# Attention in blocks of 64 queries, with two heads to an operand, and the last two operands of the recurrent projection split in place

## The chip, the cores and the metric

The kernel runs on one core of a Trainium2 chip. The metric is the device time of one execution in microseconds (us); before and after are compared by medians of several runs. In the profile the engines are called PE (TensorE, matrix multiplication; PEld is its weight load), DVE (VectorE), ACT (ScalarE), POOL (GpSimd) and SP (the engine that only issues transfers). Transfers (DMAs) between the core's memory (SBUF) and the device's memory (HBM) are issued from the queues of SP, POOL and, rarely, ACT. TensorE writes its results to PSUM.

## What is computed

One residual block of a decoder on 1024 tokens of width 1024, all in float32. Cut to what matters here:

```python
proj = h @ w_in[l]
q, k, v, g_attn, xr, g_rnn, m_attn, m_rnn = jnp.split(proj, SPLIT_POINTS, axis=-1)
# q: 16 heads of 64, k and v: 4 heads of 64; both q and k are rotated by position
s = jnp.einsum('bnqkgd,bnskd->bnkgqs', qb, kb) * (1.0 / math.sqrt(hd))
band = (diff >= 0) & (diff < WINDOW)            # a query sees itself and 127 keys before
s = jnp.where(mask[None, :, None, None], s, -1e30)
m = jnp.maximum(jnp.max(s, axis=-1, keepdims=True), sink)
p = jnp.exp(s - m)
denom = jnp.sum(p, axis=-1, keepdims=True) + jnp.exp(sink - m)
o = jnp.einsum('bnkgqs,bnskd->bnqkgd', p / denom, vb)
...
y_rnn = rg_lru(xr, ...) * jax.nn.silu(g_rnn)    # a linear recurrence over the tokens
merged = (jax.nn.sigmoid(m_attn) * (y_attn @ w_attn_proj[l])
          + jax.nn.sigmoid(m_rnn) * (y_rnn @ w_rnn_proj[l]))
x = x + gate[:, None, :] * (merged @ w_out[l])
return rmsnorm(x, final_g)
```

## The kernel before

Every float32 product is made of three: each operand is split into a high piece (a copy in the type float32r, made on ACT) and a low piece (the remainder, a subtraction on DVE), and high x high, high x low and low x high are summed in PSUM. The names end in `h` and `l` (`hh`, `hl`, `wh`, `wl`, `yh`, `yl`).

The order of the work on each engine is written by hand: the program text is the order of each queue, SP's and POOL's too. An engine that meets an instruction whose input isn't there waits, and all that follows on it waits too.

First come the normalization and the values' projection. Then `run` (L818) walks through 23 `pairs` of 256 output columns of the input projection, seven slots each, every slot 12 matmuls of 512 columns. What becomes of a pair's result is told by its "sinks": queries and keys are rotated, split and stored to HBM (`rope_a` L603, `rope_b` L620, which holds the pieces in tiles `rhi` and `rlo` of two buffers each); merge gates go through tanh and are stored (`tanh_sinks` L792); the recurrent input is convolved and goes through `after_gates` (L1003), whose steps `a1` to `d7` end in `y`, split and stored in `yh_d`, `yl_d` for each of eight channel blocks c (two to each `hb`, 0 to 3). Work that isn't tied to a slot waits in three lists (`waiting`, L651) and is put in where DVE and ACT have room by their declared costs: among it `v_prep` (L1190), which splits the values and stores them in `vs_d` and `dv_d` (the latter holds the difference of a block of 128 tokens and the one before), and `out_weights` (L1159), eight blocks of four steps that prepare the weights of the last product in the tiles `wq`. What of these is left when the attention begins goes to `rest_out` (L1593) and is put in by `outs` (L1596).

When slot 155 of the last pair is done, the attention starts: a loop over u = 0 to 34 (L1626). A unit u is 128 queries of one group of four heads that share a key head; eight units make a group, and the first of each (u % 8 == 0) has no keys before its own. The pass u of the loop emits, in this order on each engine: the scores of unit u (`scores` L1264, PE), their copy (`maxima_a`, ACT), the masked copy and the maximum (`maxima_d`, DVE), the exponentials of unit u-1 (`weights_a`, ACT), a piece of other TensorE work (what is left of the last pair, then the projection of the recurrent branch in `rp_steps` L1411: 12 matmuls of 512 columns in either case), the division (`weights_d`, DVE), the values of unit u-3 (`values` L1338, PE, with `join_a` on ACT and `join_d` on DVE), the transposes of the weights of unit u-2 (PE) and their split (`split_a` ACT, `split_d` DVE), and the masked copies of the two pieces (`masks` L1326, POOL). PSUM holds one buffer each for scores, transposes and values.

Scores of a unit are four heads x two terms: the stationary operand is one head's 128 queries (high and low pieces stacked to 128 rows), the moving operand 256 keys. The window is kept in a circular layout: the weights of the 256 keys are folded to 128 columns, key j of the block before and key j of the own block never being seen by the same query. So values are `vs` of the block before with the whole weights, and the difference `dv` with the masked ones:

```python
prods = [((vs if n else dv)[:, n % 2, :], m) for m in full]
prods += [(dv[:, n % 2, :], m) for m in masked]
```

each a matmul of 512 columns (four heads x 128 queries): four for a unit, two for a group's first.

The projection of the recurrent branch takes `y` from HBM by `load_y` (L1394), c = 0, 1 into tiles that held operands of the pairs (`hh[0..3][0]`), c = 2 to 5 into `whole`, c = 6, 7 into a pool of its own. After the loop follow the rest of this projection, the attention's projection, the merge and the last product. The tail works on the same tiles in both versions.

## Time and profile before

| what | us |
|---|---|
| three runs | 909.07, 910.93, 910.11 |
| median | 910.11 |
| the profiled run, its time | 909.08 |
| the profiled run, its span in the trace | 907.4 |

The span is what the trace covers; the 1.7 us around it are start and end. The profile's page gives, for each engine, busy time and share of the span; then the span in 40 slices; the queues; the chain of work that ended last, followed back from the last instruction; the costliest groups of instructions. Views of the trace by group, by tile, by window and in order of time give the rest. A line such as `L1274 PE MATMUL s_ps<-ks,qs 128*128 128x256` names the line of the kernel, engine, operation, output and inputs, and the shape. The ends of matmuls in the trace are modelled, so their starts and counts say more than their busy time. Loop and stages in the profiled run: pairs from 91.7 us, attention loop from 560.4 us to about 732 us, the rest to 907.4.

### The profile page before, as it was taken

Reading aid. Unit: us, or ns where it says so; the run is one execution under the profiler, and the core shown is the slowest. Engines: PE = TensorE matmul, PEld = TensorE weight load, DVE = VectorE, ACT = ScalarE, POOL = GpSimd, SP = SyncE. Lnnn points to the kernel's source line nnn. Section 1 sums busy time; section 2 is a strip of 40 time slices with the busy share of each in tenths; the row PEclk is TensorE's granted clock in tenths of the full one; section 3 lists DMA queues with packets and bytes.
Section 4 is the critical chain, followed back from the end, with each engine's and each line's share of the span. In section 5 each row is a group of like instructions: output and inputs, shape, how many; then the busy total and the mean of one; then the engine's idle time right before and its main releaser. Section 6 shows DMA issues by size and latency. Waiting matters only on the chain.

```text
span 907.4 us, 12605 instructions
## 1 busy us (share of the span) xinstructions
PE 889.1 (98%) x4171; PEld 739.2 (81%) x4171; DVE 725.8 (80%) x1158; ACT 554.9 (61%) x1097; POOL 124.7 (14%) x204
## 2 busy tenths in 40 slices
PE   5999999999999999999999999999999999999997
PEld 3879888878888788878887888888888888888885
DVE  7988799698669974987698476899999846779875
ACT  6754675455556745774767685888888731114555
POOL 0120000000110000000100001354443421310002
PEclk9999999999999999999999999999999999999999
DMA  9951786862534360345345257996666258879314
GB/s 348 404 203 68 253 272 223 294 219 97 180 121 151 130 218 24 129 155 180 107 155 183 85 194 254 328 370 211 214 201 212 85 182 322 315 272 346 110 47 186
DMA packets 88882, 182.57 MB, mean 201 GB/s; under 512 B 14049, under 2 KB 30433, under 8 KB 88818
## 3 DMA queue, kind: packets, MB, share of 16 engines
q1 hardware_dynamic: 82192, 162.09, 51.8%
q0 software_dynamic: 6336, 19.37, 5.9%
q8 instruction: 33, 0.54, 0.3%
q10 hardware_dynamic: 290, 0.32, 0.1%
q14 instruction: 31, 0.25, 0.1%
HBM read 125.01 MB, written 57.12 MB: 201 GB/s over the span
## 4 chain that ended last, share of the span: by engine, by line
PE 86%; DVE 6%; DMA 3%; ACT 2%; issue 2%; SPq 0%; POOL 0%; DVEq 0%; ACTq 0%
PE bk L696 41%; PE rp L174 14%; PE bo L1857 7%; PE pmain L174 6%; PE pgate L992 5%; PE s_ps L1274 3%; PE pv L1346 3%; DMA r<-w_main 2%; PE pt L1312 2%; PE bk L174 1%; DVE wl L110 1%; PE bk L1520 1%; PE bk L1519 1%; PE bk L1518 1%; DMA wada<-w_ss 1%
## 5 line engine op out<-in xcount | busy, mean ns | idle before, releaser
L696 PE MATMUL bk<-nh,wl 128*128 128x512 f32 x368 | 143.9, 391 | 0.5 <-DVE wl L110 0.4
L696 PE MATMUL bk<-nh,wh 128*128 128x512 f32 x368 | 143.4, 390 | 0.0
L696 PE MATMUL bk<-nl,wh 128*128 128x512 f32 x368 | 143.2, 389 | 0.0
L696 PEld LDWEIGHTS bk<-nh,wl 128*128 128x128 f32 x368 | 69.1, 188 | 16.7 <-DVE wl L110 2.1
L696 PEld LDWEIGHTS bk<-nh,wh 128*128 128x128 f32 x368 | 69.1, 188 | 14.4 <-ACT rhi L626 0.2
L696 PEld LDWEIGHTS bk<-nl,wh 128*128 128x128 f32 x368 | 69.1, 188 | 14.4
L110 DVE TENSOR_TENSOR wl<-r,wh 128x512 fp32r<-128x512 f32 x112 | 80.1, 729 | 0.0
L60 POOL DMA_DIRECT2D wq_d<-wq x32 | 21.9, 685 | 407.2 <-DVE wq L1172 392.6
L104 ACT CAST wh<-r 128x512 fp32r<-128x512 f32 x112 | 68.0, 617 | 8.8 <-DMA r<-w_ap 5.1
L696 PE MATMUL bk<-hh,wh 128*128 128x512 f32 x184 | 71.6, 389 | 0.0
L696 PE MATMUL bk<-hh,wl 128*128 128x512 f32 x184 | 71.6, 389 | 0.0
L696 PE MATMUL bk<-hl,wh 128*128 128x512 f32 x184 | 71.6, 389 | 0.0
L110 DVE TENSOR_TENSOR wl<-ws,wh 128x512 fp32r<-128x512 f32 x80 | 54.8, 686 | 4.3 <-ACT wh L104 4.2
L104 ACT CAST wh<-ws 128x512 fp32r<-128x512 f32 x80 | 48.2, 614 | 3.3 <-PE bk L1520 2.7
L1298 ACT ACTIVATE p<-p,small 128x129 f32<-128x129 f32 x128 | 50.1, 401 | 0.0
L799 ACT ACTIVATE c<-bk 128x512 f32<-128x512 f32 x31 | 18.5, 595 | 44.0 <-PE bk L696 43.9
L696 PEld LDWEIGHTS bk<-hl,wh 128*128 128x128 f32 x184 | 34.5, 188 | 7.2
L696 PEld LDWEIGHTS bk<-hh,wl 128*128 128x128 f32 x184 | 34.5, 188 | 7.1
L696 PEld LDWEIGHTS bk<-hh,wh 128*128 128x128 f32 x184 | 34.5, 188 | 7.1
L1857 PE MATMUL bo<-wh,sum 128*128 128x512 f32 x128 | 39.6, 389 | 0.0
L1274 PE MATMUL s_ps<-ks,qs 128*128 128x256 f32 (+1 forms) x256 | 37.6, 289 | 0.0
L696 PE MATMUL bk<-hha,wl 128*128 128x512 f32 x92 | 36.1, 393 | 0.6 <-DVE wl L110 0.6
(409 smaller groups left out, 2290.1 us busy)
## 6 DMA issues: line engine op xcount, KB each, us to landing
r<-w_main SPq DMA_DIRECT2D x100, 256.0 KB, 4.3
wada<-w_ss SPq DMA_DIRECT2D x16, 512.5 KB, 9.3
qs<-q_d SPq DMA_DIRECT2D x16, 512.0 KB, 5.8
wq_d<-wq POOLq DMA_DIRECT2D x24, 256.0 KB, 2.8
wr<-wq_d SPq DMA_DIRECT2D x24, 256.0 KB, 5.0
ks<-k_d SPq DMA_DIRECT2D x24, 192.0 KB, 4.2
wq<-w_out POOLq DMA_DIRECT2D x16, 256.0 KB, 5.2
q_d<-rhi SPq DMA_DIRECT2D x16, 256.0 KB, 3.6
```

The costliest lines, as they stand in the source:

```text
L60: return eng.dma_start(dst, src)
L104: A.copy(dst[0][:], src)
L110: V.tensor_tensor(out=dst[1][:], in0=src, in1=f32(dst[0][:]), op=ALU.subtract)
L174: mm = T.matmul(ps[hf], ww, xx[kc][hf], start=(kc == 0 and ww is w_h and xx is xh), stop=(kc == KC - 1 and xx is xl))
L696: W["pe"] = T.matmul(ps, ww[:, c], b[kc][xx_], start=(first and kc == 0 and i == 0), stop=(kc == 3 and i == 2), skip_group_check=not first)
L799: A.activation(t["t"], s(), AF.Tanh, scale=0.5)
L992: W["pe"] = T.matmul(ps[:, SL[hf]], ww[:, c0:c0 + P], xx_[:, SL[hf]], start=(ic == 0 and i == 0), stop=(ic == 1 and i == 2))
L1274: W["pe"] = T.matmul(o, qs[:, j, qc], ks[:, b, k0 + (0 if n else P):k0 + 256], start=(b == 0), stop=(b == 1))
L1298: A.activation(px[:, j, :], px[:, j, :], AF.Exp, bias=sm[:, 0, j:j + 1], accum_out=sm[:, 1, j:j + 1])
L1312: W["pe"] = T.transpose(pt[:, j, :], px[:, j, 0:P], ident[:])
L1346: W["pe"] = T.matmul(pv[:], b, m[:].rearrange("p j q -> p (j q)"), start=(i == 0), stop=(i == len(prods) - 1))
L1857: T.matmul(bank[p][i] if dst is None else dst, a[:, ts_], b[:][:, sl], start=(new and kc == 0 and j == 0), stop=(kc == 3 and j == 2), skip ...
```

## The change

It has two parts.

The attention works in blocks of 64 queries. A unit is still 128 queries of four heads, but a stationary operand of the scores holds two heads x 64 queries, and its moving operand is the 192 keys that these can see (`h` is the half of the unit). Weights are folded to 128 columns, of which only 64 need the mask. In the values, a matmul has 256 columns (two operands of one half): four with the whole weights' pieces, and two with `cm`, in which the masked 64 rows of the high and of the low piece are stacked. The first unit of a group leaves out those that see no keys. For this, queries lie in HBM by blocks of 64 tokens (`q_d`) and are stored from POOL's queue in runs of 64 floats, values lie by blocks of 64 with two blocks of zeros in front (`vs_d`), and four transfers from POOL's queue load them instead of two. The merge gates' stores are all issued from POOL.

In the last two blocks of the recurrent branch (c = 6, 7), `y` isn't split and stored: `d6` writes it into the four tiles `wq`, and `y_direct` splits it into `hh`, `hl` just before and in the first pass of the attention loop. For that, `out_weights` stops after three of its eight blocks, and the load of the fourth comes at u = 26 from SP. The pieces of the recurrent projection's first two columns run over c = 6, 7, then 4, 5, then 0 to 3, and `load_y` follows that order. The tiles `yq` of the loop take turns on one tile of their own and two of `wq`.

Not shown: the mask of 64 columns in place of 128, the sinks' layout, the split of `load_kq` into `load_k` and `load_q`, and index changes in the joins.

```diff
-    vs_d = [tc.dram_tile([P, 8, P], F32, name=f"vs_d{g}") for g in range(NG)]
-    dv_d = [tc.dram_tile([P, 8, P], F32, name=f"dv_d{g}") for g in range(NG)]
+    vs_d = [tc.dram_tile([64, 18, P], F32, name=f"vs_d{g}") for g in range(NG)]
+    dv_d = [tc.dram_tile([64, 18, P], F32, name=f"dv_d{g}") for g in range(NG)]
...
-    q_d = [tc.dram_tile([512, S], F32, name=f"q_d{g}") for g in range(NG)]
+    q_d = [tc.dram_tile([16, 512, 64], F32, name=f"q_d{g}") for g in range(NG)]
...
+    zero = rpp.tile([P, HALF], F32, tag="rl", name="zero", bufs=2)
+    G.memset(zero[:, :2 * P], 0.0)
...
+    for g in range(NG):
+        dma(vs_d[g][:, 0:2, :], zero[0:64, :2 * P].rearrange("p (i c) -> p i c", i=2), G)
...
-            dma(dst[r0:r0 + P, SL[th]], t["h"][:])
-            dma(dst[r0 + 2 * P:r0 + 3 * P, SL[th]], t["l"][:])
+            for n_, r in ("h", r0), ("l", r0 + 2 * P):
+                if dst is k_d:
+                    dma(dst[r:r + P, SL[th]], t[n_][:])
+                else:
+                    dma(dst[8 * th:8 * th + 8, r:r + P, :].rearrange("x p q -> p x q"),
+                        t[n_][:].rearrange("p (x q) -> p x q", q=64), G)
...
-                        dma(dst[j][:, SL[th]], t["t"], G if "att" in W else nc.sync)
+                        dma(dst[j][:, SL[th]], t["t"], G)
...
+            if hb < 3:
+                V.tensor_tensor(out=t["rz"][:], in0=t["rz"][:], in1=t["gg"][:], op=ALU.mult)
+                return
+            for i in range(2):
+                V.tensor_tensor(out=wq[2 * oc + i][:].rearrange("p a t -> p (a t)"),
+                                in0=t["rz"][:, SL[i]], in1=t["gg"][:, SL[i]], op=ALU.mult)
...
+                [[("D", 0, 1.22, d6)]]] + ([[], []] if hb == 3 else [
+                    [[("A", 1.05, 0, a7)]], [[("D", 0, 1.22, d7)]]])
...
+                if (kc, q) == (1, 1):
+                    waiting[2].append(lambda: False)
                 waiting[2].extend(out_weights(kc, slice(q * 256, q * 256 + 256)))
...
                 dma(t[:], w_out[k * P:(k + 1) * P, :].rearrange(
-                    "p (a t) -> p a t", a=2)[:, :, cols], G)
...
-                dma(dst[g], t[d_][:])
+                for b in range(2):
+                    dma(dst[g][:, 2 + b:18:2, :], t[d_][64 * b:64 * b + 64])
...
+        dma(qs[:], q_d[g][t0 // 64:t0 // 64 + 4].rearrange("x (a j) q -> a x (j q)", j=4))
+        U["q", m] = qs
...
-        g, n0 = m // 4, (m % 4) * 2
-        vs = at.tile([P, 2, P], F32R, tag="vs", name="vs", bufs=2)
-        dv = at.tile([P, 2, P], F32R, tag="dv", name="dv", bufs=2)
-        dma(dv[:], dv_d[g][:, n0:n0 + 2, :], G)
-        lo = 0 if n0 else 1
-        dma(vs[:, lo:, :], vs_d[g][:, n0 - 1 + lo:n0 + 1, :], G)
-        U["v", m] = vs, dv
+        g, i0 = m // 4, m % 4 * 4
+        vb = at.tile([P, 4, P], F32R, tag="vb", name="vb", bufs=2)
+        vd = at.tile([P, 4, P], F32R, tag="vd", name="vd", bufs=2)
+        for e in range(2):
+            half = slice(64 * e, 64 * e + 64)
+            dma(vb[half], vs_d[g][:, i0 + e:i0 + e + 4, :], G)
+            dma(vd[half], dv_d[g][:, i0 + 2:i0 + 6, :], G)
+        U["v", m] = vb, vd
...
-        qc = slice((n % 2) * P, (n % 2 + 1) * P)
-        k0 = (n % 2) * P
+        ks, qs = U["k", u // 2], U["q", u // 2]
         s_full = psx.tile([P, 1024], F32, tag="s", name="s_ps")
         s_ps = s_full[:].rearrange("p (j k) -> p j k", j=4)
         for j in range(4):
-            o = s_ps[:, j, :] if n else s_ps[:, j, P:]
+            h = j // 2
+            t0 = (n % 2) * P + 64 * h
+            first = 0 if n else P - 64 * h
+            w = qs[:, n % 2 * 2 + h, j % 2 * P:j % 2 * P + P]
             for b in range(2):
-                W["pe"] = T.matmul(o, qs[:, j, qc], ks[:, b, k0 + (0 if n else P):k0 + 256],
+                W["pe"] = T.matmul(s_ps[:, j, first:192], w, ks[:, b, t0 + first:t0 + 192],
                                    start=(b == 0), stop=(b == 1))
         U["s", u] = s_ps, *U.pop(("p", u))
         if n % 2 and u // 2 + 2 < 16:
-            load_kq(u // 2 + 2)
+            load_k(u // 2 + 2)
+            load_q(u // 2 + 2)
...
         s_ps, px, sm = U["s", u]
-        A.copy(px[:, :, 0:P], s_ps[:, :, P:])
+        if u % 8:
+            A.copy(px[:, :, 0:P], s_ps[:, :, 0:P])
+        else:
+            A.copy(px[:, :, 0:64], s_ps[:, :, P:192])
...
-        p = px[:, :, 0:P]
+        p = px[:, :, 0:64]
         if u % 8:
-            V.copy_predicated(p, W["mgt"][:].unsqueeze(1).to_broadcast([P, 4, P]),
-                              s_ps[:, :, 0:P])
+            V.copy_predicated(p, W["mle"][:].unsqueeze(1).to_broadcast([P, 4, 64]),
+                              s_ps[:, :, P:192])
         else:
-            G.affine_select(out=p, in_=p, pattern=[[0, 4], [-1, P]], compare_op=ALU.is_ge,
-                            fill=-1e30, base=0, channel_multiplier=1)
+            G.memset(px[:, 0:2, 64:P], -1e30)
+            for e in range(2):
+                o = p[64 * e:64 * e + 64]
+                G.affine_select(out=o, in_=o, pattern=[[0, 4], [-1, 64]],
+                                compare_op=ALU.is_ge, fill=-1e30, base=0,
+                                channel_multiplier=1)
...
     def masks(u):
-        phc, plc = U["m", u]
-        ms = []
-        if u % 8:
-            for s_, tag in ((phc, "phm"), (plc, "plm")):
-                d_ = at.tile([P, 4, P], F32R, tag=tag, name=tag)
-                G.affine_select(out=d_[:], in_=f32(s_[:]), pattern=[[0, 4], [1, P]],
-                                compare_op=ALU.is_ge, fill=0.0, base=0,
-                                channel_multiplier=-1)
-                ms.append(d_)
-        U["m", u] = [phc, plc], ms
+        pieces = U["m", u]
+        cm = at.tile([P, 4, P], F32R, tag="cm", name="cm")
+        for i, s_ in enumerate(pieces):
+            G.affine_select(out=cm[64 * i:64 * i + 64].rearrange("p g (e q) -> p (g e) q", e=2),
+                            in_=f32(s_[0:64]).rearrange("p g (e q) -> p (g e) q", e=2),
+                            pattern=[[0, 8], [1, 64]], compare_op=ALU.is_ge, fill=0.0, base=0,
+                            channel_multiplier=-1)
+        U["m", u] = *pieces, cm
...
-        n = u % 8
-        vs, dv = U["v", u // 2]
-        full, masked = U.pop(("m", u))
-        prods = [((vs if n else dv)[:, n % 2, :], m) for m in full]
-        prods += [(dv[:, n % 2, :], m) for m in masked]
-        pv = psx.tile([P, 4 * P], F32, tag="v", name="pv")
-        for i, (b, m) in enumerate(prods):
-            W["pe"] = T.matmul(pv[:], b, m[:].rearrange("p j q -> p (j q)"),
-                               start=(i == 0), stop=(i == len(prods) - 1))
-        U["pv", u] = [pv[:].rearrange("p (a e q) -> p a e q", a=2, e=2)]
-        if n % 2 == 0 and u // 2 + 1 < 16:
+        vb, vd = U["v", u // 2]
+        phc, plc, cm = U.pop(("m", u))
+        pv = psx.tile([P, 4, P], F32, tag="v", name="pv")
+        prods = [(vb, m, h) for m in (phc, plc) for h in range(0 if u % 8 else 1, 2)]
+        prods += [(vd, cm, h) for h in range(2)]
+        for i, (b, m, h) in enumerate(prods):
+            js = slice(2 * h, 2 * h + 2)
+            W["pe"] = T.matmul(pv[:, js, :], b[:, u % 2 * 2 + h, :], m[:, js, :],
+                               start=(i == 0), stop=(i >= len(prods) - 2),
+                               skip_group_check=True)
+        if u % 2 == 0 and u // 2 + 1 < 16:
             load_v(u // 2 + 1)
...
-            W["yq"] = at.tile([P, 2, 256], F32, tag="yq", name="yq", bufs=3)
+            W["yq"] = (at.tile([P, 2, 256], F32, tag="yq", name="yq") if u % 6 == 0 else
+                       wq[1 + u % 6 // 2])
...
+    def y_direct(c):
+        j = 2 * (c - 6)
+        yh[c], yl[c] = [[t[j + i][0] for i in range(2)] for t in (hh, hl)]
+        for i in range(2):
+            src = wq[j + i][:].rearrange("p a t -> p (a t)")
+            later_a.append(lambda i=i, src=src: A.copy(yh[c][i], src))
+            later_d.append(lambda i=i, src=src: V.tensor_tensor(
+                out=yl[c][i], in0=src, in1=f32(yh[c][i]), op=ALU.subtract))
+
+    Y_ORDER = (4, 5, 0, 1, 2, 3)
+
+    def load_y(n):
+        c = Y_ORDER[n]
+        if n < 4:
+            h_, l_ = whole["hh", n + 4], whole["hl", n + 4]
...
             for kc in (2 * kc2, 2 * kc2 + 1):
                 W["pe"] = mm_k([rp_acc[c % 2][:, t] for t in SL], (O.get((c, 0)), O.get((c, 1))),
-                               kc, xh=yh, xl=yl)
+                               kc, xh=yh, xl=yl, first=0 if c > 1 else 6,
+                               last=KC - 1 if c > 1 else 3)
...
-        seq = [(c, k) for k in range(4) for c in range(2)]
+        seq = [(c, k) for k in (3, 2, 0, 1) for c in range(2)]
         seq += [(c, k) for c in range(2, KC) for k in range(4)]
-        load_y(3)
+        load_y(1)
...
             if i in (0, 1, 2, 3):
-                load_y(i + 4)
...
-    at_slot(s_last + 2, [("N", 0, 0, lambda: load_r(0)), ("N", 0, 0, lambda: load_y(0))],
-            ("N", 0, 0, lambda: load_y(1)), ("N", 0, 0, lambda: load_r(1)), [],
-            [("N", 0, 0, lambda: prep_r(0, 0)), ("N", 0, 0, lambda: load_y(2))],
-            ("N", 0, 0, lambda: prep_r(1, 0)))
+    y_direct(6)
+    do_later()
+    at_slot(s_last + 2, [("N", 0, 0, lambda: load_r(0)), ("N", 0, 0, lambda: y_direct(7))],
+            [], ("N", 0, 0, lambda: load_r(1)), [],
+            [("N", 0, 0, lambda: prep_r(0, 1)), ("N", 0, 0, lambda: load_y(0))],
+            ("N", 0, 0, lambda: prep_r(1, 1)))
...
+            if u == 0:
+                load_k(1)
+                load_q(1)
+                load_v(0)
...
+        if u == 26:
+            outs(1)
```

More of the change, by code (lines that the diff above doesn't have):

```diff
@@ L174, in mm_k @@
                 mm = T.matmul(ps[hf], ww, xx[kc][hf],
[L175 to L176 removed]
+                              start=(kc == first and ww is w_h and xx is xh),
+                              stop=(kc == last and xx is xl))
         return mm
@@ L1644, in tile_hybrid_block @@
             join_a(u - 3)
+        if u >= 3:
             join_d(u - 3)
```

77 lines of the change are left out of this document (38 added, 39 removed).

## The prediction

> **What bounds the kernel.** The page's busy table comes first, then its chain of waits by engine: TensorE is busy for nearly the whole span, and most of the chain that ends last runs through it.
>
> ```profile
> PE 889.1 (98%) x4171; PEld 739.2 (81%) x4171; DVE 725.8 (80%) x1158; ACT 554.9 (61%) x1097; POOL 124.7 (14%) x204
> PE 86%; DVE 6%; DMA 3%; ACT 2%; issue 2%; SPq 0%; POOL 0%; DVEq 0%; ACTq 0%
> ```
>
> Busy time of pipelined matmuls is no measure of a stage, so I read the chain in order of time where the change works: the loop over 32 units (u = 0 to 31; four of them, u = 0, 8, 16, 24, are the first of their group). Columns: start us, length us, group.
>
> ```profile
> 672.06 0.95 PE s_ps L1274 x8
> 673.01 2.75 PE rp L174 x12
> 675.75 0.91 PE pv L1346 x4
> 676.66 0.44 PE pt L1312 x4
> 677.10 0.84 PE s_ps L1274 x8
> 677.94 2.82 PE rp L174 x12
> 680.77 0.91 PE pv L1346 x4
> 681.68 0.44 PE pt L1312 x4
> 682.11 0.95 PE s_ps L1274 x8
> ...
> 695.90 0.46 PE pv L1346 x2
> ```
>
> One pass is scores (0.95), a piece of the projection (2.75), values of an earlier unit (0.91) and transposes (0.44): 672.06 to 677.10 is 5.04 us, the four pieces sum to 5.05, and nothing is between them. The unit at 677.10 is a first one, with 128 score columns instead of 256; the 0.46 at 695.90 is a first unit's values, two matmuls instead of four. So here time is TensorE's own work, and what the change takes from it counts, as long as the others keep up. The view by stages (us; busy and count for PE, PEld, DVE, ACT, POOL; clock, DMA share, GB/s) says how near they are:
>
> ```profile
> 663.00:688.00 25.00, 25.00 (x141) 21.52 (x140) 22.95 (x43) 19.94 (x66) 13.72 (x22) 1.00 0.61 193
> ```
>
> DVE 92%, ACT 80%, POOL 55%. The clock is 1.00: no gain or loss from there.
>
> **Values.** A 512-column matmul costs 0.91 / 4 = 0.228 us, a 256-column one 0.95 / 8 = 0.119. Four of the first become six of the second (two halves with each of the high and low pieces, two with the masked pieces stacked into one operand): 6 x 0.119 = 0.714, a gain of 0.197, of which I take 0.19. A first unit goes from 0.46 to 4 x 0.119 = 0.476, a loss of 0.02.
>
> **Scores.** Eight matmuls remain, of 192 columns instead of 256. By the rows, eight of 128 columns cost 0.84 (0.105 each), so below 256 columns the pitch hardly falls: the weight load of each sets it. And the first unit doesn't keep even that: its projection piece is 2.82 instead of 2.75, so the two together are 3.66 against 3.70, a gain of 0.04. With 192 columns the gain lies between 0 (the 256 row) and 0.11 (the 128 row, without the late projection). I take 0.03, near what the whole 128-column unit showed. The first units' scores are short already: nothing.
>
> Here the Trainium skill has two rules ("TensorE: Matmul & The Clock Gate"). Its section "Back-to-back issue gap" gives a warm matmul N / 2.4 + 2.5 ns, an estimate of 82 ns for 192 columns; its section "LDWEIGHTS (loading the stationary operand)" gives 128 columns of weights 128 / 1.2 = 107 ns. The trace agrees with the second (0.105), which speaks against this part of the change; by the first alone it would gain 8 x (0.119 - 0.082) = 0.29 per unit.
>
> **Does the gain reach the end?** The loop drains at its end:
>
> ```profile
> 716.97 0.03 ACTq L1317
> ...
> 719.45 1.03 POOL plm L1332
> 720.48 0.04 issue
> 720.52 0.50 PE pv L1346
> ```
>
> From 716.97 to 720.52 TensorE waits for one unit's copy, split and mask; three of its four values matmuls run in that gap and only the last is exposed. Afterwards four of six do and two are exposed, so that unit's values gain nothing. Sum: 27 x (0.19 + 0.03) + 0.03 - 4 x 0.02 = 5.9 us.
>
> **What must keep up.** Groups by form between 607 and 688 us (busy us, mean ns, idle before and its cause), and two of one tile (shortest, median, longest ns) for the slope by size:
>
> ```profile
> L1288 DVE COPY_PREDICATED p<-mgt,s_ps 128x512 f32<-128x512 uint32 x15 | 11.1, 738 | 0.0
> L1293 DVE TENSOR_REDUCE small<-p 128x4 f32<-128x516 f32 x17 | 11.7, 691 | 3.0 <-POOL p L1291 1.1 <-DVE p L1288 0.5
> L1355 ACT COPY ob<-pv 64x256 f32<-64x256 f32 x17 | 6.3, 369 | 14.0 <-PE pv L1346 6.5 <-issue 6.1 <-ACT p L1298 1.5
> L1332 POOL TENSOR_SCALAR_AFFINE_SELECT plm<-plc 128x512 fp32r<-128x512 f32 x14 | 14.0, 1002 | 9.3 <-DVE plc L1323 9.3
> L1332 POOL TENSOR_SCALAR_AFFINE_SELECT phm<-phc 128x512 fp32r<-128x512 f32 x14 | 9.1, 652 | 11.3 <-ACT phc L1317 11.3
> L60 POOL DMA_DIRECT2D dv<-dv_d x8 | 4.4, 554 | 0.0
> ...
> L1172 DVE TENSOR_TENSOR wq<-wq,gate_bc x16: 682/689/694, 232.6 to 798.3; 128x512 f32<-128x512 f32 x16
> L1177 DVE TENSOR_TENSOR wq<-wq x8: 417/420/424, 235.6 to 798.9; 128x256 f32<-128x256 f32 x8
> ```
>
> The new pass is 5.04 - 0.22 = 4.82. DVE's masked copy of the scores halves its columns and, by the slope 689 - 420, loses 0.27: DVE goes from 0.92 x 5.04 = 4.63 to 4.36, 90% of the new pass. ACT keeps its 4.02 (0.80 x 5.04), 83%, and stood idle 14.0 us over 17 units for the join copy, 0.8 each, against the 0.22 that go. POOL's two masks keep 512 elements per partition, on half the partitions; a bound of 0 and of the longer row, 1.0, each. It gets four loads of values instead of two in every second unit, 2 x 0.55 = 1.1 us, and in each first unit two masks that weren't there (1.65) and three short operations for one: 2.8 of a pass at 55% becomes 3.3 of 4.82. What counts is when the mask is ready:
>
> ```profile
> 649.37 1.02 POOL L1332 TENSOR_SCALAR_AFFINE_SELECT plm<-plc 128x512 fp32r<-128x512 f32 x1 [0.37 <-DVE plc L1323]
> 651.50 0.39 PE L1346 MATMUL pv<-plm,dv 128*128 128x512 f32 x1
> ```
>
> It ends at 650.39 and is used at 651.50: 1.1 us of cover, more than the 0.22. So none of these costs anything; with the cover gone each us of lateness would be paid 32 times.
>
> **What moves.** The last two operands (channels 6 and 7) lose two stores and two loads each way through memory, and two ACT and two DVE operations in the recurrent stage; four ACT copies and four DVE subtractions of 512 columns (0.69 each) come at the loop's start, 2.8 us on DVE. That engine waits there:
>
> ```profile
> 562.85 0.69 DVE L1293 TENSOR_REDUCE small<-p 128x4 f32<-128x516 f32 x1 [5.40 <-POOL p L1291]
> ```
>
> 5.4 us idle before it covers them: nothing, at most 0.7 for one that comes late. The other operands keep their distance to their use (the order of loads and of the pieces is permuted together). Of the output weights only one load moves, from POOL in mid-kernel to SP at unit 26, long before its use: nothing.
>
> **Queues.** Queries (32 stores) and merge-gate stores leave SP's queue for POOL's, and query stores become runs of 256 bytes, 1024 in a store. SP's view, then two slices by stages, a wait and issue times:
>
> ```profile
> 163.90 5.58 SPq L60 DMA_DIRECT2D sma_d<-c  x2
> 169.53 0.93 SPq L60 DMA_DIRECT2D r<-w_main  x2
> ...
> 170.00:180.00 10.00, 10.00 (x46) 8.29 (x45) 6.30 (x20) 3.94 (x8) 0.00 (x0) 1.00 0.98 339
> 180.00:190.00 10.00, 9.83 (x41) 7.17 (x40) 9.52 (x17) 6.16 (x11) 0.00 (x0) 1.00 0.38 135
> ...
> 131.78 0.38 SPq L60 DMA_DIRECT2D q_d<-rhi  x1
> 146.76 0.32 SPq L60 DMA_DIRECT2D q_d<-rhi  x1
> ...
> L60 POOL DMA_DIRECT2D wq_d<-wq x32: 562/725/742, 233.6 to 800.7; - x32
> ACT rhi L626 <- DMA q_d<-rhi: 8.9, 4, 4.1
> ```
>
> On the good side: weight loads that stood behind two waiting gate stores went out at 169.53, and in 180 to 190 TensorE started 41 matmuls, not 46: 5 x 0.228 = 1.1 us that may go. On the bad side: POOL takes 0.56 us for a store of 128 runs and 0.74 for one of 256, so 1024 runs are, as an estimate, 0.56 + 7 x 0.18 = 1.8 us; no row shows such a store on POOL (bounds 0.56 and, at twice the slope, 3.1). Eight of them, one group's, take 14.6 us, and two groups start 131.78 and 146.76, 15.0 us apart: it just fits. Behind a late store wait ACT and DVE, which need its two buffers back, as ACT does already (8.9 us in four times), and behind them the weights. I take 0 for both together (bounds: 1.1 gained, 15 lost).
>
> **Sum.** The profiled run took 909.08 (span 907.4); the median of three, 910.11, is 1.0 above it. 909.08 - 5.9 = 903.2, and from the median **904.2**.
>
> **The rivals.**
> 1. *The scores run at column rate.* Columns cost (0.228 - 0.119) / 256 = 0.42 ns, so 192 would be 0.092, eight 0.73, a gain of 0.22 per unit instead of 0.03: 28 x 0.19 = 5.3 more, 899. The 128-column row speaks against it. The first rule of the Trainium skill's TensorE page, above, would bring 28 x (0.29 - 0.03) = 7.3 more, an estimate of 897.
> 2. *The cover is gone.* DVE at 90% is late by pieces (its slowest operations meet POOL's masks), or the mask comes after its use; half to all of the gain is lost: 906 to 910. For it: DVE and ACT feed each other in one pass. Against: DVE gains more than TensorE.
> 3. *Slower: POOL can't issue the query stores.* The point is 15.0 / 8 = 1.9 us a store. At 2.7, 24 stores of three groups are 19 us late, of which the idle share of DVE and the buffers hide perhaps a third: +13, 917. For it: the estimate lies just below the point. Against: POOL has nothing else there (0.00 busy in both slices). The Trainium skill ("SBUF — State Buffer", section "SBUF: two separate sides") says that descriptors written by GpSimd are blocked while DVE holds the shared port, 0.62 us becoming 3.1. By it such a store would pass the point easily; the trace's 32 POOL stores, 0.74 at the longest, don't show it.
> 4. *It doesn't do what it says*: the loop's pass stays 5.04, 910.
>
> **Chances.** Forecast, 901 to 906: 0.62. Rival 1 or the 1.1 us and a better start, below 901: 0.11. Rival 2: 0.13, half of it within 0.2% (1.8 us, about what a measurement of this kernel can tell from no change). Rival 3: 0.12. Rival 4: 0.02. Faster 0.80, same 0.08, slower 0.12. The range 899.5 to 908.0 leaves out rival 3, the slow end of rival 2 and a little below.
>
> **What would show it.** In the profile after, a pass of 4.8 us with eight scores at 0.85 to 0.95, six values at 0.71 and transposes at 0.44, and nothing between them. Right as to SP: 46 matmuls in the slice where 41 were. Wrong: gaps between values and transposes, waits of TensorE on DVE or POOL in the loop; POOL's query stores over 1.9 us with waits of ACT on rhi and DVE on rlo; a pass near 4.6 (rival 1).

## The result, and the profile after

The kernel after takes 914.67 us (median of 12 runs, 911.68 to 918.14), the kernel before in the same comparison 909.02 (12 runs, 907.43 to 910.93): a ratio of 1.0061, 95% interval 1.0045 to 1.0077. It is 5.6 us slower where 5.9 us faster was forecast. The profiled run took 912.4 us, 2.3 below its median, with a span of 910.7. The runs of the kernel after differ by 6.5 us, those of the kernel before by 3.5, and the longer ones have the lower granted clock: 0.998 in the run of 911.68, 0.991 in that of 918.14.

The same views as before the change, first the page's busy table and its chain by engine. (Lines have moved: scores are L1304, values L1383, transposes L1351, matmuls of the pairs L706.)

```profile
PE 885.6 (97%) x4235; PEld 739.1 (81%) x4235; DVE 720.3 (79%) x1162; ACT 554.5 (61%) x1103; POOL 191.8 (21%) x313
PE 60%; issue 12%; DVE 12%; DMA 7%; ACT 5%; POOL 4%; SPq 1%; DVEq 0%; POOLq 0%; ACTq 0%
```

TensorE's share of the chain falls from 86 to 60%; "issue" rises from 2 to 12%, DVE from 6 to 12, the transfers (DMA) from 3 to 7, ACT from 2 to 5 and POOL from 0 to 4. Yet the pass that was forecast is there, in the chain in order of time (start, length, group) and in the view by stages:

```profile
653.12 0.87 PE s_ps L1304 x8
653.99 2.77 PE rp L174 x12
656.76 0.72 PE pv L1383 x6
...
657.91 0.87 PE s_ps L1304 x8
...
661.55 0.47 PE pv L1383 x4
...
663.00:688.00 25.00, 25.00 (x156) 22.24 (x156) 22.73 (x43) 21.89 (x70) 15.12 (x28) 1.00 0.83 240
```

653.12 to 657.91 is 4.79 us, against 5.04; the values take 0.72, a first unit's 0.47, the scores 0.87. So the loss is elsewhere. To find it, take the start of the scores of each unit from TensorE's timeline; three of the 32 for the kernel before, then for the one after:

```profile
560.19 1.00 PE L1274 MATMUL s_ps<-ks,qs 128*128 128x128 f32 x8
621.86 1.19 PE L1274 MATMUL s_ps<-ks,qs 128*128 128x256 f32 x8
711.67 1.19 PE L1274 MATMUL s_ps<-ks,qs 128*128 128x256 f32 x8
```
```profile
564.93 1.00 PE L1304 MATMUL s_ps<-ks,qs 128*128 128x64 f32 x8
628.60 1.12 PE L1304 MATMUL s_ps<-ks,qs 128*128 128x192 f32 x8
715.51 1.12 PE L1304 MATMUL s_ps<-ks,qs 128*128 128x192 f32 x8
```

They are units 0, 13 and 31. "Passes 0 to 12" is the time from the first to the second of them, "13 to 30" from the second to the third. The forecast's sum (0.19 for a unit's values, 0.03 for its scores, -0.02 for a first unit's values), cut at the same places, stands beside it:

| stretch | before | after | change | forecast |
|---|---|---|---|---|
| up to the first scores | 560.2 | 564.9 | +4.7 | 0 |
| passes 0 to 12 | 61.7 | 63.7 | +2.0 | -1.8 |
| passes 13 to 30 | 89.8 | 86.9 | -2.9 | -3.5 |
| the rest of the span | 195.7 | 195.2 | -0.5 | -0.6 |

The last two rows came nearly as forecast. 9.2 us separate the profiled time from the sum, and 8.5 of them lie in the first two rows: 4.7 before the loop, 3.8 in its first thirteen passes. Each has its own cause. (The medians lie further apart than these two profiles: 5.6 us slower, not 3.3. The rows place what the profiled run lost; they don't hold the 2.3 us between it and its median.)

**Before the loop.** The stages of after, where the kernel before had 46 and 41 matmuls, and TensorE's timeline in the second of them:

```profile
170.00:180.00 10.00, 9.67 (x43) 8.01 (x44) 6.86 (x21) 4.49 (x9) 1.08 (x2) 1.00 0.77 227
180.00:190.00 10.00, 7.68 (x27) 5.85 (x26) 7.49 (x14) 4.60 (x9) 0.26 (x1) 0.83 0.55 194
```
```profile
181.12 0.39 PE L706 MATMUL bk<-nh,wh 128*128 128x512 f32 x1
183.82 0.50 PE L706 MATMUL bk<-nh,wl 128*128 128x512 f32 x1 [2.32 <-DVE wl L112]
...
185.32 0.63 PE L706 MATMUL bk<-nh,wl 128*128 128x512 f32 x1
...
188.73 0.39 PE L706 MATMUL bk<-hha,wh 128*128 128x512 f32 x1
```

TensorE waits 2.32 us for the low piece of a weight, and then, from 185.32 to 188.73, eight matmuls start 0.43 us apart instead of 0.227. Back along the chain that weight is `DMA r<-w_main`, issued at 175.48. SP's view around it, before and then after:

```profile
170.55 0.38 SPq L60 DMA_DIRECT2D vs_d<-vs  x1
171.05 0.35 SPq L60 DMA_DIRECT2D dv_d<-dv  x1
...
173.78 0.98 SPq L60 DMA_DIRECT2D r<-w_main  x1
```
```profile
170.90 1.27 SPq L60 DMA_DIRECT2D vs_d<-vs  x2
172.26 1.63 SPq L60 DMA_DIRECT2D dv_d<-dv  x2
...
175.48 2.54 SPq L60 DMA_DIRECT2D r<-w_main  x2
```

The split values go to HBM in four transfers instead of two, in runs of 512 bytes. They occupy SP for 3.0 us instead of 0.9, and the weight load behind them goes out 1.7 us later. From there to its landing it takes 7.0 us, and 6.6 before: it comes late because it is issued late. The queries' stores, which the prediction feared, take POOL 0.89 us each.

**In the loop's first passes** the chain runs through value loads, here the third pair of units:

```profile
591.12 0.57 POOL smr_d L60
591.68 0.53 POOL vb L60
592.21 0.52 POOL vd L60
...
593.23 9.06 DMA vd<-dv_d
...
602.42 0.49 PE pv L1383 x2
```

Four issues stand behind a merge-gate store on POOL, and the last of them lands 9.06 us later. Where TensorE waits in the loop (total us, times, longest), where the kernel before has one wait of 0.3 us:

```profile
PE pv L1383 <- POOL cm L1369: 1.4, 3, 0.7
PE pv L1383 <- DMA vb<-vs_d: 1.2, 1, 1.2
```

Two more, for `vd` and for a result of DVE, take 0.3 us each.

### The profile page after: what moved, and what is told of

Same layout as the page of the kernel before. It is cut to its first block, busy times and chain, and to the rows that moved or that the text cites. A ratio compares the mean times of both kernels' runs of the same rounds, so it can differ in the third digit from the quotient of the medians.

```text
span 910.7 us, 12963 instructions
## 1 busy us (share of the span) xinstructions
PE 885.6 (97%) x4235; PEld 739.1 (81%) x4235; DVE 720.3 (79%) x1162; ACT 554.5 (61%) x1103; POOL 191.8 (21%) x313
## 2 busy tenths in 40 slices
DMA packets 92917, 183.12 MB, mean 201 GB/s; under 512 B 14561, under 2 KB 39649, under 8 KB 92850
## 4 chain that ended last, share of the span: by engine, by line
PE 60%; issue 12%; DVE 12%; DMA 7%; ACT 5%; POOL 4%; SPq 1%; DVEq 0%; POOLq 0%; ACTq 0%
PE bk L706 26%; PE rp L174 12%; PE bo L1913 7%; PE pmain L174 5%; PE pgate L1002 5%; PE s_ps L1304 2%; DMA r<-w_main 2%; DVE wl L110 2%; PE pv L1383 2%; POOL q_d L60 2%; DMA wg<-posi 1%; DVE jk L251 1%; DMA vd<-dv_d 1%; PE pt L1351 1%; DVE ws L728 1%
## 5 line engine op out<-in xcount | busy, mean ns | idle before, releaser
L706 PE MATMUL bk<-nh,wl 128*128 128x512 f32 x368 | 144.6, 393 | 4.6 <-DVE wl L112 2.3
L706 PE MATMUL bk<-nl,wh 128*128 128x512 f32 x368 | 143.8, 391 | 0.0
L706 PE MATMUL bk<-nh,wh 128*128 128x512 f32 x368 | 143.7, 391 | 0.0
L706 PEld LDWEIGHTS bk<-nh,wl 128*128 128x128 f32 x368 | 69.2, 188 | 21.8 <-DVE wl L110 5.0
L706 PEld LDWEIGHTS bk<-nh,wh 128*128 128x128 f32 x368 | 69.2, 188 | 14.4
L706 PEld LDWEIGHTS bk<-nl,wh 128*128 128x128 f32 x368 | 69.4, 188 | 14.2
L706 PE MATMUL bk<-hh,wh 128*128 128x512 f32 x184 | 71.7, 389 | 0.0
L706 PE MATMUL bk<-hl,wh 128*128 128x512 f32 x184 | 71.6, 389 | 0.0
L706 PE MATMUL bk<-hh,wl 128*128 128x512 f32 x184 | 71.6, 389 | 0.0
L706 PEld LDWEIGHTS bk<-hh,wl 128*128 128x128 f32 x184 | 34.6, 188 | 7.3
L706 PEld LDWEIGHTS bk<-hh,wh 128*128 128x128 f32 x184 | 34.5, 188 | 7.1
L706 PEld LDWEIGHTS bk<-hl,wh 128*128 128x128 f32 x184 | 34.5, 188 | 7.1
L706 PE MATMUL bk<-hha,wl 128*128 128x512 f32 x92 | 36.3, 394 | 0.9 <-DVE wl L110 0.9
L706 PE MATMUL bk<-hha,wh 128*128 128x512 f32 x92 | 36.0, 392 | 0.0
```

Of the source, the lines that this page charges most:

```text
L706: W["pe"] = T.matmul(ps, ww[:, c], b[kc][xx_], start=(first and kc == 0 and i == 0), stop=(kc == 3 and i == 2), skip_group_check=not first)
```

## Experiments

Three theories for the first row of the table: V (value stores), Q-runs (256-byte runs of the query stores), Q-queue (POOL's queue for queries and gates). Three for the second: I (POOL's issue order and time), B (the doubled bytes of the value loads), L (loads issued too late); a fourth, Y (late loads of y), came up on the way. "First scores" and passes are read as above, from one profiled run each; times are medians, ratios are to runs of the kernel before on the same chip. Some profiles are of runs far from their median: e1's took 5.1 us more (914.95), e16's 4.6 less (906.33), e18's 1.5 more, and e4's 10.9 more, a run that its ratio leaves out; their stages are read with that in mind. e6, e10 and e17 leave out half of the values, so they are measures of a cause and not kernels to use. Of those that do the whole computation `e12_all` is the fastest. Runs on different chips are compared by their ratios.

| kernel | us | ratio (95%) | first scores | passes 0-12 | 13-30 |
|---|---|---|---|---|---|
| e1_v_store | 909.85 | 1.0002 (0.9980-1.0024) | 559.8 | 69.4 | 87.0 |
| e2_q_runs | 917.5 | 1.0097 (1.0069-1.0125) | 562.3 | 69.0 | 86.9 |
| e3_queues | 916.51 | 1.0073 (1.0047-1.0099) | 565.3 | 66.1 | 86.8 |
| e4_v_two | 962.47 | 1.0551 (1.0481-1.0622) | 568.6 | | |
| e5_v_early | 914.25 | 1.0052 (1.0037-1.0067) | 559.6 | 63.4 | 93.0 |
| e6_v_half | 906.96 | 0.9969 (0.9955-0.9983) | 559.2 | 62.2 | 87.0 |
| e7_v_two | 965.88 | 1.0595 (1.0547-1.0643) | 562.6 | | |
| e8_v_end | 909.2 | 0.9992 (0.9975-1.0008) | 558.7 | 65.0 | 87.1 |
| e9_v_pool | 908.73 | 0.9988 (0.9972-1.0004) | 558.2 | 63.8 | 87.3 |
| e10_half_end | 905.73 | 0.9956 (0.9940-0.9973) | 560.4 | 61.2 | 87.0 |
| e11_y_early | 909.97 | 1.0000 (0.9986-1.0013) | 558.7 | 65.6 | 87.0 |
| e12_all | 906.41 | 0.9970 (0.9959-0.9981) | 558.9 | 61.9 | 87.0 |
| e13_y | 908.49 | 0.9995 (0.9981-1.0009) | 559.1 | 65.3 | 87.0 |
| e14_end | 910.48 | 1.0012 (1.0000-1.0024) | 560.3 | 65.7 | 87.3 |
| e15_y_late6 | 907.47 | 0.9985 (0.9971-0.9999) | 560.0 | 62.5 | 86.9 |
| e16_y_undone | 910.95 | 1.0029 (1.0015-1.0043) | 558.3 | 63.6 | 86.9 |
| e17_all_half | 905.92 | 0.9959 (0.9945-0.9973) | 558.4 | 61.9 | 87.0 |
| e18_before_dose | 911.16 | 1.0013 (1.0002-1.0023) | 561.7 | 63.6 | 89.8 |

### The time before the loop: e1, e2, e3, e9

e1: values in HBM by whole blocks of 128 tokens again, one store each; a pair of units then needs five loads instead of four (not shown).

```diff
...
-                for b in range(2):
-                    dma(dst[g][:, 2 + b:18:2, :], t[d_][64 * b:64 * b + 64])
+                dma(dst[g][:, 1:9, :], t[d_][:])
...
```

> Of the 4.7 us that are lost before the attention loop (first scores at 560.35 before, 565.09 after). Value stores again in one transfer of 4 KB runs each (eight issues on SP instead of sixteen), five loads of values instead of four. Theory V (the stores of v in 512-byte runs hold SP and the transfers, so v and w_main land late): first scores at 561 to 562, 46 matmuls in 160-190, time 4 us under after, about 910. Theory Q (the query stores, their runs or their queue): first scores stay at 564 to 566, time that of after, 914 to 916 (the fifth load may cost some 0.5 in the loop).

e2: queries in runs of 2 KB; four transfers load them instead of one (not shown).

```diff
...
-                    dma(dst[8 * th:8 * th + 8, r:r + P, :].rearrange("x p q -> p x q"),
-                        t[n_][:].rearrange("p (x q) -> p x q", q=64), G)
+                    dma(dst[r:r + P, SL[th]], t[n_][:], G)
...
```

> Queries stored in runs of 2 KB again, still from POOL's queue; the loads take the 256-byte runs instead, four transfers for one, from SP in the loop. Theory Q-runs (256-byte runs in the stores load the transfers where queries are made): first scores at 561 to 562. Theory Q-queue (POOL's queue instead of SP's) and theory V: stay at 564 to 566. In the loop the loads may cost something; the total is then no better than after, the first scores decide.

e3: `G` taken from these stores and, up to the attention, from the merge gates'.

> Query stores (still 256-byte runs) and merge-gate stores from SP's queue again. Theory Q-queue: first scores at 560 to 562 and 4 us under after, about 910. Theories Q-runs and V: 564 to 566, 914 to 916.

Only e1 starts the loop as early as the kernel before. (e2's time is no measure here: TensorE waits 3.6 us for one of its query loads in the loop.) e3, with all the old queues, has the same event as after; its chain:

```profile
175.63 6.81 DMA r<-w_main
...
183.07 0.69 DVE wl L112
...
183.81 11.38 PE bk L706 x36
```

Q-queue falls with e3, and e2's 562.3 leaves Q-runs at most a part. But the first scores also hold what the profiled runs differ by ahead of this event: the 673rd matmul of the pairs starts at 169.73 us before, at 168.14 in after and at 170.84 in e18, which changes nothing there. The time from it to the start of the 757th leaves that out. It is 20.11 us before, 24.71 in after, 19.72 in e1, 22.72 in e2 and 24.88 in e3, so e2 keeps most of the loss too. V stays, but e1 changed both the issues and the packets. e9 takes the four stores as they are and issues them from POOL (`G` at the end of the two lines).

> After, with the four stores of values per group (512-byte runs as in after) issued from POOL's queue instead of SP's. Theory V-issue (what counts is SP's time for four issues, 0.6 us each and up, ahead of the weight loads r<-w_main): first scores at 560 to 561.5, no wait of TensorE at 183, time 909 to 911. Theory V-packets (the 512-byte packets fill the transfers and the weights land late whoever issues them): first scores at 563 to 566, time 913 to 916.

The stages of e9:

```profile
160.00:170.00 10.00, 10.00 (x46) 8.29 (x45) 8.23 (x19) 5.02 (x10) 3.86 (x7) 1.00 0.93 308
170.00:180.00 10.00, 10.00 (x46) 8.29 (x45) 8.56 (x25) 4.24 (x8) 3.26 (x5) 1.00 0.98 314
180.00:190.00 10.00, 10.00 (x46) 8.29 (x45) 9.93 (x18) 7.57 (x15) 2.67 (x3) 1.00 0.62 216
```

46 matmuls in each, and the first scores at 558.2, 2.0 us ahead of the kernel before. All profiles agree: the 84 matmuls from the 673rd to the 757th take 22.40 to 24.88 us in the five with four value stores on SP (after, e2, e3, e4, e7), 19.25 to 20.40 in the eight with two, and 19.04 in each of the seven with four on POOL.

That the stores have to leave SP is shown. e9 alone doesn't show that it is SP's time and not the packets, since the packets changed as well: on POOL's queue these stores go in packets of 4096 bytes, and the kernel's packets under 2 KB fall from 39649 to 31457. Two other things speak for SP's time. The weight load is late in after, not slow: from its issue to its landing it takes 7.0 us, in e3 and e9 6.8, before 6.6. And e3, whose query stores add some 25000 packets under 512 bytes between 100 and 200 us (29517 against 4414), loses what after loses. Whether four stores hold SP that long by their number or by their shorter runs, no run separates.

### The value loads: e4, e7, e5, e6, e8

e4 and e7: two loads of 128 partitions, whose source is written out by hand (two halves, 64 partitions each); e7 joins the 2 KB of a partition in the target, too.

```diff
-        for e in range(2):
-            half = slice(64 * e, 64 * e + 64)
-            dma(vb[half], vs_d[g][:, i0 + e:i0 + e + 4, :], G)
-            dma(vd[half], dv_d[g][:, i0 + 2:i0 + 6, :], G)
+        for t_, d_, i_, step in (vb, vs_d, i0, P), (vd, dv_d, i0 + 2, 0):
+            o = d_[g][:, i_:i_ + 4, :]
+            dma(t_[:], bass.AP(o.tensor, o.offset, [[step, 2], [18 * P, 64], [1, 4 * P]]), G)
```

> Values loaded by two transfers of 128 partitions instead of four of 64, same bytes, still from POOL. Theory I (the loop's 4.6 us are lost at its start by POOL: four issues of 0.53 stand ahead of the masks cm, and the last lands 9 us later): loop (first scores to last values) 2 to 3 us shorter than the 170.3 of after, waits of TensorE in 580-620 half as long, time 912. Theory B (the loads' doubled bytes, 8 instead of 4 MB, against transfers that are busy all the time): loop as long as in after, within 0.7. First scores at 564 to 566 by both.

> After, with two value loads of 128 partitions in place of four of 64, and now in runs of 2 KB (e4_v_two had made 512-byte packets of them, 26000 in the software queue instead of 12176, and landed in 12.5 us). First scores at 564 to 566 as in after. Theory I: loop 2 to 3 us shorter than the 170.3 of after, time 911 to 912. Theory B: loop within 1 of after, 914 to 915. If 512-byte packets were what was wrong with e4_v_two, its 962 is gone by both.

Both miss: 50 us slower. The view of the tile `vb` in e7 says why the question wasn't reached:

```profile
DMA to landing us min/median/max: 7.7/12.5/18.4
```

Nearly twice the 6.8 of after for twice the bytes in one transfer, so the values come late: in e7 TensorE waits 27.7 us for `vb`, in seven times, and 8.7 for `vd`. e7's edit didn't change the packets either (26000 in the software queue in both), and those that e4 and e7 have more than after are all under 512 bytes, not of 512 as I had expected. The Trainium skill ("DMA: Bandwidth & Descriptors", section "Rules for kernel authors") says that a source whose outermost dimension has c < 16 entries confines a transfer to at most c of the 16 engines; here c is 2. No run here shows whether that is the cause: no view counts the engines, the small packets are another candidate, and 256 KB in 12.5 us is about the rate of one of after's transfers (128 KB in 6.8 us).

e5: on e1, the load that followed the values of an even unit follows those of the odd unit before.

```diff
...
-        if u % 2 == 0 and u // 2 + 1 < 16:
-            load_v(u // 2 + 1)
+        if u % 2 and u // 2 + 2 < 16:
+            load_v(u // 2 + 2)
...
```

> On top of e1_v_store, the loads of values are issued one pass earlier (behind the values of the odd unit, as soon as their buffer is free). Theory L (the loop loses its time because the value loads, 5 to 10 us from issue to landing when the transfers are busy, come too late for the second pass after their issue): no wait of TensorE for vb or vd, no slice of lower clock in 580-630, loop 164 to 166 us, time 903 to 905. Theory I (the time that POOL spends on issuing, ahead of the masks cm): the loads stand ahead of the masks as before, so TensorE goes on waiting; gain under 1.5, time 908 to 910.

e6: on e1, every value load cut to two of its four slots.

> e1_v_store with half of each value load left out (slots 0 and 1 of four are loaded and used for all), five issues as before, none earlier. Theory B (the doubled bytes, 8 instead of 4 MB, make the loads land late): median landing 4 to 5 us instead of 6.1 to 6.3, no wait for vb or vd, time 903 to 905. Theory I (issue time on POOL): loads are issued as late as before and the masks wait behind them; time 907 to 910.

e8: as e5, but called at the end of the pass, behind `masks(u - 2)`.

> As e5_v_early, but the loads stand behind the masks of the pass instead of ahead of them. If both lateness and order on POOL count, this is the fastest: no wait for vb or vd and fewer waits of TensorE for cm (2.9 us in 7 and 1.4 in 3 in after), time 902 to 904. If only lateness counts, equal to e5_v_early within 0.5. If neither, 908 to 910.

e5 took away every wait for a value load and still ran at 914.25, because the five issues of a pair (2.9 us by their means) now stood ahead of masks on which the next pass hangs. TensorE's waits in its loop (total us, times, longest):

```profile
PE pv L1389 <- POOL cm L1375: 8.9, 13, 1.7
```

So I is real, but it is a matter of place. e8 waits for no value load and only 1.2 us for the masks, and got two new waits:

```profile
PE s_ps L1310 <- DMA qs<-q_d: 2.2, 1, 2.2
PE rp L174 <- DMA yl<-yl_d: 1.6, 1, 1.6
```

Its chain:

```profile
583.87 12.97 DMA hl<-yl_d
...
596.86 12.04 DMA yl<-yl_d
...
608.92 13.07 DMA yl<-yl_d
...
622.03 0.72 PE rp L174 x2
```

From 584 to 622 the chain runs through loads of y that take 12 to 13 us each. e6 against e1 (0.9969 to 1.0002, about 3 us) says that bytes count. What the transfers moved in 545 to 565 and in 565 to 635 us, in the kernel before and in e8, whose loops begin within 1.5 us of each other:

```profile
DMA packets 3152, 4.85 MB, mean 242 GB/s; under 512 B 407, under 2 KB 1943, under 8 KB 3150
...
DMA packets 12378, 21.41 MB, mean 306 GB/s; under 512 B 1163, under 2 KB 8359, under 8 KB 12370
```
```profile
DMA packets 1487, 2.76 MB, mean 138 GB/s; under 512 B 200, under 2 KB 876, under 8 KB 1484
...
DMA packets 12041, 21.04 MB, mean 301 GB/s; under 512 B 1326, under 2 KB 8484, under 8 KB 12034
```

In the view by stages the DMA share of the second stretch is 0.92 before (306 GB/s) and 1.00 in e8 (301); e8 comes to it with 2.1 MB less done. These rates aren't the most that is seen: e18, below, moves 338 GB/s in the same stretch. The tiles in which the kernel before received blocks 0 and 1 of y at the loop's start are now those in which `y_direct` splits blocks 6 and 7, and the other loads have to wait for tiles that come free some 15 to 20 us later (first load of y issued at 558.48 before, at 573.09 in e8 and at 579.34 in after).

### Bytes, y and order: e10, e11, e12, e13, e14

e10 is e8 with e6's cut.

> e8_v_end with half of each value load left out as in e6_v_half: value stores as before, loads a pass earlier and behind the masks, half the bytes. If the transfers (bytes) and POOL's order are all that took the gain of the loop, the loop falls from the 171.6 us of e8_v_end to 165.5 to 167 and the time to 902.5 to 904.5, the forecast. If another cause (DVE, ACT) holds the loop's start, the loop stays above 168.5 and the time above 906.

Its 905.73 lies between the two: half the bytes bring 3.3 us (0.9992 to 0.9956), and passes 0 to 12 still take 61.2 us where the forecast's sum leaves 59.9.

e11, on e8: block 4 is loaded early, block 6 split late.

```diff
...
-    y_direct(6)
+    y_direct(7)
     do_later()
-    at_slot(s_last + 2, [("N", 0, 0, lambda: load_r(0)), ("N", 0, 0, lambda: y_direct(7))],
+    at_slot(s_last + 2, [("N", 0, 0, lambda: load_r(0)), ("N", 0, 0, lambda: load_y(0))],
...
```

> e8_v_end with all loads in full; y of block 4 is loaded at the loop's start, when the transfers are half idle (into the tiles that y_direct(6) took), and block 6 is split in place later, two passes before its use; 1 MB leaves the stretch 577-630. Theory B: waits for qs and yl (2.2 and 1.6 us in e8_v_end) shrink, loop 168 to 170, time 905 to 907. If the transfers aren't the bound there, the time stays at 909, or rises by the 1.3 us that DVE and the 1.1 us that ACT get to do in two passes of 580-595.

e11 traded one wait for another: TensorE waited 1.9 us for the split of block 6, which came one pass before its use. e12 to e14 are on e9; e12 splits block 6 sooner and loads three more blocks as soon as their tiles are free; e13 is e12 without the change to the value loads, e14 has only that change.

```diff
...
+            [("N", 0, 0, lambda: load_y(1)), ("N", 0, 0, lambda: y_direct(6, (0,)))],
+            [("N", 0, 0, lambda: prep_r(0, 1)), ("N", 0, 0, lambda: load_y(2)),
+             ("N", 0, 0, lambda: y_direct(6, (1,)))],
+            [("N", 0, 0, lambda: prep_r(1, 1)), ("N", 0, 0, lambda: load_y(3))])
...
```

> e9_v_pool, with the loads of values a pass earlier and behind the masks (as e8_v_end), and with y brought in sooner: block 4 loaded at the loop's start, 5, 0 and 1 as soon as their tiles are free (up to two passes before after's order), block 6 split in place three and two passes before its use. Theory Y (the transfers are full in 570-630 because the loads of y start 20 us later than in the kernel before: 2.9 MB in 545-565 against 4.85, 21 MB in 565-635 in both): no wait of rp for yl or hh, loop 165.5 to 168, time 902.5 to 905.5. If something else takes the loop's start, loop above 169.5 and time 907 to 909.

> The same without the change to the loads of values (they stand ahead of the masks, as in after). If the sooner y alone frees the transfers, the value loads land in time too: loop 166 to 169, time 903 to 906. If the order on POOL is needed as well: waits for cm and vb remain (1.8 and 2.2 us in e9_v_pool), loop 169 to 171, time 906 to 908.5.

> e9_v_pool with only the change to the loads of values. Theory Y: the wait moves to the loads of y and of queries as in e8_v_end, loop 170 to 172, time 907 to 909.5. If POOL's order is what counts: loop 166 to 168.5, time 903.5 to 906.

Neither alone brings anything: by the ratios e13 is 0.6 us slower than e9 and e14 2.2. Both together are 2.3 us faster than e13 and 3.8 faster than e14, clear of noise; against e9 they bring 1.6 us, which the intervals don't separate. e12's 906.41 lies between the two expectations for it. In e13 the sooner y collides with the value loads, in e14 the sooner values collide with y; one chain row of each:

```profile
577.36 10.42 DMA vd<-dv_d
```
```profile
611.15 13.13 DMA yl<-yl_d
```

### What is left: e15 to e18

e15: block 6 split two passes later. e16: on e14, the part on y undone. e17: e12 with e6's cut. e18: the kernel before with two more transfers, memory to memory, behind each pair of value loads.

```diff
...
+        for i, d_ in enumerate((dv_d, vs_d)):
+            dma(more_d[2 * m + i], d_[g][:, n0:n0 + 2, :], G)
```

> e12_all, but block 6 is split two passes later (and the first pieces of the projection run over blocks 4, 5 before 6, 7). In e12_all some 3 us are still missing in 580-600, where its chain runs through ACT and DVE, the split of block 6 among it. If that split is the cause: more than 60 matmuls in each of 580-590 and 590-600 (53 and 58 in e12_all), loop 166 to 167.5, time 904 to 905.5. If the last pair's own results on ACT and DVE are the cause: unchanged within 0.7, 906 to 907.

> The part on y undone in e14_end: blocks 6 and 7 are stored and loaded like the others, loads of y start in the loop's first pass with blocks 0 and 1 and follow in the order of the kernel before; the attention's part, the value stores on POOL and the value loads a pass earlier stay. Theory Y (the late loads of y decide, not the doubled bytes of the values): no chain through yl and hl, loop 166.5 to 169 although 2 MB more are loaded, time 904.5 to 907. If the values' bytes decide: 2 MB more make it worse, loop 172 to 174, time 909 to 911.

> e12_all with half of each value load left out (two of four slots loaded and used). If the 3 us that e12_all lacks are again the transfers: loop 165.5 to 167, time 903 to 904.8, where the prediction had it. If they are work on ACT and DVE in the loop's first passes: loop within 0.7 of the 168.5 of e12_all, time 905.5 to 907.

> The kernel before, with the bytes of its value loads doubled and nothing else: behind each pair of loads two more of the same size go from memory to memory, from POOL's queue, nobody waits for them. Theory B (the bytes in the full stretch cost time by themselves): loop 173 to 176 instead of 171.4, waits for value, query or y loads in 580-630, time 911 to 914. If the kernel before has room for them: 908.5 to 910.

e18: 1.2 us more in the median (911.16 against 909.92; interval of the ratio 1.0002 to 1.0023) for the doubled bytes and their issues; in its profiled run, 1.5 us above the median, passes 0 to 12 take 1.9 us more, passes 13 to 30 nothing. So bytes cost by themselves, but a third to a half of the 3.8 us lost there. e16 is no better than e14, though its y starts as early as before (5.19 MB moved in 545 to 565 us): theory Y as I had put it, that lateness decides and not the bytes, falls. e16 moves 2.1 MB more than e14 in 545 to 565 us and 1.2 MB more in 565 to 635, e14 starts its loads later: the two cost about the same (1.0029 and 1.0012, intervals that overlap). e17 gains nothing in the passes over e12, so the 2 us that e12 still lacks there (61.9 where 59.9 was forecast) aren't the bytes of the values. TensorE waits for no transfer in e12's loop:

```profile
PE pv L1383 <- POOL cm L1369: 1.0, 3, 0.4
PE rp L174 <- ACT u L755: 0.9, 1, 0.9
```

Its chain from 576 to 605 us runs mostly through ACT and DVE, which prepare the last pair of the projection, split y and do the attention at once; e15 moved one part of it and was no faster (0.9985 against 0.9970). No run took work from these two engines, so that this is the rest is argued, not shown.

## Why the prediction was wrong

- **Values**: right. 0.72 and 0.47 were forecast as 0.714 and 0.476.
- **Scores**: the reason was right, the size a little low: 0.87 / 8 = 0.109 each, 0.08 gained per unit in the chain's rows instead of 0.03. Rival 1 didn't happen. The pitch agrees with the 107 ns of a weight load in the Trainium skill ("TensorE: Matmul & The Clock Gate", section "LDWEIGHTS (loading the stationary operand)"), not with the 82 ns estimated from its section "Back-to-back issue gap".
- **The sum past the start**: passes 13 to 30 and all that follows gained 3.4 us of 4.1. What is missing are some passes at 4.9 to 5.1 us among those of 4.8; in the one that starts at 667.25 the scores take 1.01 us and the values 0.81. No run looked for the cause.
- **What must keep up**: right for the steady pass (DVE 91%, forecast 90; ACT 88% rather than 83), wrong for the start. "So none of these costs anything" took the four value loads as 1.1 us of POOL's time and left out two things: they carry twice the bytes into a stretch (565 to 635 us) whose DMA share was 0.92 before, and on POOL they stand between a gate store and the masks. Doubled in the kernel before, the bytes and their issues cost 1.2 us (e18); half of them left out brings about 3 us in e6 and e10.
- **What moves**: the step that failed here is "the other operands keep their distance to their use". Counted in passes they do; in time their loads start later, in the stretch that was nearly full already. What that costs shows in e14 and e12, which differ only in how and when y comes in: 3.8 us. That the part on y as a whole cost nothing, as forecast, was luck: e16, without it, moves more and is no faster than e14. Of the 3.8 us lost in passes 0 to 12, e12, which mends the order of the value loads and the lateness of y, gets 1.8 back; the cause of the other 2.0 stays open.
- **Queues**: the step that failed before the loop. I weighed the query stores and the gate stores against each other and took 0; the estimate of 1.8 us for a query store was twice too high (0.89 at the median, 0.94 at most), and rival 3 fell with it. The 3.1 us of the Trainium skill ("SBUF — State Buffer", section "A bandwidth-pool intuition that's wrong (but worth ruling out)") aren't seen. But the edit that I quoted in the diff and priced nowhere, two value stores made four, holds SP 2.1 us longer ahead of a weight load and costs 4.6 us over the 84 matmuls measured above (24.71 against 20.11). The good side was there as well: with those stores off SP they take 19.04 us, which is the 1.1 us that the prediction saw as possible. The rest of the 2.0 us by which e9's loop starts sooner was there ahead of them and is no gain of the change.
- **Range and rivals**: the one slower rival ended at 917, near the time, by a mechanism that the runs exclude. Rival 2 was nearest to the truth, but at the loop's start and by transfers and POOL's order rather than in the steady pass.

## What to carry to other kernels

Price every transfer that an edit adds or splits on the queue that issues it, with the first load that stands behind it, also where the edit seems to be about another stage. A gain per pass is safe only where the pass is TensorE's own; where a loop starts beside the end of another stage, add up the bytes of that stretch against what the transfers moved there before. When two versions are compared by one profile each, measure the stage from its own start, because the runs can differ ahead of it (here by up to 2.7 us). And a wait that is removed in a nearly full stretch comes back one tile further on: e5, e8, e11, e13 and e14 each removed one and met the next, and only two changes together (e12, 0.9970 of the time before) paid.

## What the hardware showed unexpectedly

- A pause of TensorE can cost more than its length. After 2.32 us, eight matmuls of 512 columns ran at 0.43 us instead of 0.227 (above). In e1 a pause of 1.98 us was followed by these rows of the chain, and by a granted clock of 0.69 in the slice:

```profile
598.46 1.56 PE pv L1389 x6
...
600.88 1.60 PE s_ps L1310 x8
602.48 4.57 PE rp L174 x12
```
```profile
600.00:610.00 10.00, 10.00 (x48) 8.85 (x47) 6.80 (x12) 6.54 (x20) 4.17 (x8) 0.69 1.05 314
```

  The values take 1.56 us instead of 0.72 and the piece of the projection 4.57 instead of 2.77: 2.6 us more in these two rows, more than the pause. The length of one pause doesn't decide it. In e3 a pause of 1.57 us (to 602.2) stands at a granted clock of 0.70 from 601 to 606 us and 0.61 to 611; in e8 one of 2.17 us (to 617.0) left the clock at 1.00, as did pauses of 1.1 to 1.2 us in after (at 170 and 601 us). The Trainium skill ("TensorE: Matmul & The Clock Gate", section "HAM oscillation — how this bites in real kernels") warns of gaps above some 3.4 us; here shorter ones were enough, but not always.
- A store of 1024 runs of 256 bytes from POOL takes 0.89 us to issue, and the trace shows it as packets of 4096 bytes. The high pieces land in 3.6 us and the low ones in 4.2 (medians of 16), where the stores of 2 KB runs from SP took 3.6 and 3.4 before. Only where SP issues the same stores, in e3, are there packets of 256 bytes (32768 more under 512 bytes than in after); they land in 4.0 and 3.3 us. The Trainium skill ("DMA: Bandwidth & Descriptors", section "Specifications") wants 512 bytes at least for the full rate; these landings show no loss, but they don't measure the rate.
- Two transfers of 64 partitions and 128 KB each land sooner than one of 128 partitions and 256 KB whose source is in two halves: 6.8 us against 12.5 (after and e7). The cause is open, as said above.
